# A transformer stack on one core: weight splits moved from the norms' powers into the modulation, one buffer for the normalised activation, five of its blocks made during V

## The chip, the cores and the metric

The kernel runs on one core of a Trainium2 chip. A time is the device time of one launch in microseconds. The kernel before has a median of 1303.39 us over three runs, from 1303.30 to 1306.41 us. The one execution that was profiled took 1308.08 us, and the span of its trace is 1306.3 us. TensorE is called PE, VectorE DVE, ScalarE ACT, GpSimd POOL, and SyncE (which issues the loads here) SP.

## The reference

256 rows of width 1024 pass through two blocks. The first has two layers of three sublayers each, and every sublayer is a norm, a modulation by vectors that come from a conditioning vector, some products, and a gated addition to the residual stream:

```python
def rms_norm(x, g): return x * rsqrt(mean(x * x, -1) + EPS) * g
def modulate(h, shift, scale): return h * (1.0 + scale) + shift
def swiglu(h, w_in, w_out):
    g, u = split(h @ w_in, 2)
    return (silu(g) * u) @ w_out
for layer in range(2):
    mods = split(silu(c) @ ada_w[layer] + ada_b[layer], 9)      # shift, scale, gate of three sublayers
    h = modulate(rms_norm(x, norm_g[layer, 0]), mods[0], mods[1])
    x = x + 0.5 * (1 + mods[2]) * swiglu(h, ffn_w_in[layer, 0], ffn_w_out[layer, 0])
    h = modulate(rms_norm(x, norm_g[layer, 1]), mods[3], mods[4])
    y = pool_mixer(h) if layer == 0 else attention(h, *kv) @ w_o  # windowed means; 8 heads of 128
    x = x + (1 + mods[5]) * y
    h = modulate(rms_norm(x, norm_g[layer, 2]), mods[6], mods[7])
    x = x + 0.5 * (1 + mods[8]) * swiglu(h, ffn_w_in[layer, 1], ffn_w_out[layer, 1])
    if layer == 0:
        k, v = split(modulate(rms_norm(x, kv_norm), *kv_mods) @ w_kv, 2)
        kv = rope(rms_norm(k)), v
```

The second block (one layer) norms and modulates x, multiplies it by a wide w_in, runs a state-space branch and a latent-attention branch, merges them with gates and adds the normed result to x.

## The kernel before, in words

**Tiling.** The residual stream X lies transposed in SBUF as eight blocks of 128 x 256 (width by rows). Every weight is cut into tiles of 128 x 1024 floats (512 KB). SP loads a tile as `wraw` (L215, five buffers); ACT rounds it to `whi` (L229) and DVE subtracts that to get the rest, `wlo` (L220). Activations are split in the same way into the two halves of `hhl`. PE then forms every block product as three: `whi` by high, `wlo` by high, `whi` by low (L355 to L358, L368 to L370). A tile's split is asked for by `Stream.split`, mostly four tiles ahead of its use.

**Modulation vectors.** Each is a product of a 512 KB tile `graw` with the conditioning vector. Most are made on DVE (`junk`, L389), a few on PE while PE would wait in a norm; the table GAPS says which three. Their results come back through three ACT copies (`grow`, L414) and a transposition (L419).

**A norm.** ACT squares the blocks of X, POOL adds them up (L484), PE sums over partitions (L500), DVE adds epsilon (`stm`, L518), POOL takes the power -1/2 (`strs`, L520), and PE spreads the result over the partitions (L526). `st_finish` (L503) does this, and between the power's issue and PE's spreading it calls `more` (L507), which splits one weight tile beyond those already asked for: `whi` on ACT and `wlo` on DVE.

**The modulation** (`modulated`, L541) takes the eight blocks in order. For a block DVE forms `hraw` (L533), ACT adds the shift and rounds (`hhl`, L534), DVE makes the low part (L538), one block behind. At block 2 ACT also makes the three `grow` copies. PE's next products take the blocks in this order.

**The order of the work** is written out by the program: each engine runs its instructions in the order in which the Python calls make them, and waits at the first whose inputs aren't there. A buffer of a pool is given out anew when its last reader is done; `hhl` comes from a pool of one buffer, so a new activation waits for the last product with the old one.

**Places.** The names of norms used below: g00 (after the first FFN, before the pool mixer), gpool (before the second FFN), g01 (before the shared keys and values), g10 (before the attention's queries), g11 (after attention), p2 (before the second block). After the values (V) the first FFN of layer 1 uses the same norm as the keys, kept in `rbs`. The head is the part up to the first FFN's products; there the first tiles and vectors (`hg`) are still being loaded.

Of the kernel before, what the change touches and what calls it, by code (L numbers as in the profile page):

```python
# [8 lines left out]
F32 = mybir.dt.float32  # L9
F32R = mybir.dt.float32r  # L10
# [3 lines left out]
OP = mybir.AluOpType  # L14
# [3 lines left out]
T = 256  # L18
KB = 8
# [46 lines left out]
def _cols(v):  # L66
# [3 lines left out]
NADA = 184  # L70
ADA_PAIR = [m * 8 + k for k in range(8) for m in (0, 1)]
ADA_LAYER = ADA_PAIR + list(range(16, 72))
GAPS = {"g00": (57, 58, 59), "gpool": (64, 65, 66), "g01": (104, 105, 106), "g10": (128, 129, 130),
        "p2": (176, 177, 178), "g11": (152, 153, 154)}
HEAD_PE = {0: (4, 6), 2: (8, 10), 4: (12, 14)}
POOL_PE = (60, 61, 62, 63)
# [174 lines left out]
class Kernel:  # L251
    def __init__(self, nc, tc, h, ctx, dbg=None):
        self.nc, self.tc, self.h, self.ctx = nc, tc, h, ctx
        self.dbg = dbg or {}
        self.bg = deque()
        self.pending = deque()
        self.budget = deque()
        self.small_q, self.small_rate, self.small_credit = deque(), 0.0, 0.0
        self.credit = 0.0
        self.calls = 0  # L260
        self.late = None
        self.lq = []

    def dump(self, name, t):
        if name in self.dbg:
# [237 lines left out]
    def st_finish(self):  # L503
        self.st_reduce()
        if self.gap:
            self.gap[0](2, 5)
            self.more()  # L507
        rb = self.st_spread()
        if self.gap:
            self.gap[0](5, 8)  # L510
        return rb
# [26 lines left out]
        self.nc.vector.scalar_tensor_tensor(a[:, kb, 1], hr, g[:, 1, kb:kb + 1], a[:, kb, 0].bitcast(F32),  # L538
                                            op0=OP.add, op1=OP.subtract)

    def modulated(self, rb, g, a):  # L541
        prev = None
        for kb in range(KB):
            hr = self.mod_a(rb, g, a, kb)
            if kb == 2 and self.gap:
                self.gap[1]()
                self.gap = None
            if prev:
                self.mod_b(*prev)
            prev = (hr, g, a, kb)  # L550
        self.mod_b(*prev)

    def newh(self):
        return self.hpool.tile([128, KB, 2, T], F32R, name="hhl")

    def update(self, kb, ps, g, eng=None, late=None):
        for i in range(0, ps.shape[1], T):
# [208 lines left out]
                                   op0=OP.mult, op1=OP.mult)  # L766
        self.ropeT = {kind: t}

    def kv_project(self, hh):
        nc = self.nc  # L770
        with self.tc.tile_pool(name="kvt", bufs=1) as self.ap:
            self.rope_table(0, "k", 128.0 ** 0.5)
            ssq = self.ap.tile([128, 8, 2], F32, name="kssq")
            pend = []

            def rope(p, nch, th):
                m1 = self.qk_rope(p, nch, th, ssq, "k")
                pend.append(lambda: self.qk_transpose(m1, self.KT, nch, th))

            def evac(nch, pp):  # L780
                while pend:
                    pend.pop(0)()
                if nch < 2:
                    for th in range(2):
                        self.qk_stats(pp[th], nch, th, ssq)
                        self.defer(rope, pp[th], nch, th, lag=1 + th)
                else:
                    for th in range(2):
                        nc.scalar.copy(self.VV[:, th, (nch - 2) * 512:(nch - 1) * 512], pp[th])
            self.proj_b(hh, 4, evac)  # L790

    def attention(self, hh, gate_fn, pre):
        nc, V = self.nc, self.nc.vector
        with self.tc.tile_pool(name="attn", bufs=1) as self.ap:
            self.rope_table(1, "q", 1.0)
            QT = self.ap.tile([128, 8, T], F32, name="QT")
            rq = self.ap.tile([128, 8, 2], F32, name="rq")
            self.shift(self.ap, 192)
            oo = self.ap.tile([128, 8, 2, T], F32R, name="ohl")
            pend = []  # L800

            def evac(nch, pp):
                while pend:
                    pend.pop(0)()
                if nch:
                    last_pp.extend(pp)
                    return
                stats(pp, nch)
                for th in range(2):
                    rope(pp[th], nch, th)  # L810

            def stats(pp, nch):
                for th in range(2):
                    self.qk_stats(pp[th], nch, th, rq)

            def rope(p, nch, th):
                m1 = self.qk_rope(p, nch, th, rq, "q")
                pend.append(lambda: self.qk_transpose(m1, QT, nch, th))
            last_pp = []
            S, P, PT = {}, {}, {}  # L820

            def rest():
                while pend:
                    pend.pop(0)()

            def s1a(h):
                S[h] = self.softmax_a(self.ps("D" if h < 2 else "A"), QT[:, h], self.KT[:, h], 0,
                                      lambda th: rq[:, h, th:th + 1], rq[:, h, :])

            def s1b(h):  # L830
                P[h] = self.softmax_b(*S.pop(h))

            def s2(h):
                PT[h] = self.p_transpose(P.pop(h))

            def s3(h):
                pt = PT.pop(h)
                po = self.ps("D")
                d = slice(h * 128, h * 128 + 128)
                nc.tensor.matmul(po[:, :256], self.VV[:, 0, d], pt[:, :256], start=True, stop=False)  # L840
                nc.tensor.matmul(po[:, 128:256], self.VV[:, 1, d], pt[:, 256:], start=False, stop=True)
                nc.scalar.copy(oo[:, h, 0], po[:, :T])
                V.tensor_sub(oo[:, h, 1], po[:, :T], oo[:, h, 0].bitcast(F32))

            mids = self.gemvs(AT_A, 152)
            first, mids, last = mids[:AT_Q], mids[AT_Q:len(mids) - AT_O], mids[len(mids) - AT_O:]
            self.plan(first, [0] * 3 + [1] * 3)
            self.proj_b(hh, 2, evac, hooks={HQ: rest, (1, 6): lambda: s1a(0)})
            self.drain()
            for it in range(1, 11):  # L850
                if it == 4:
                    rest()
                if it < 8:
                    s1a(it)
                if it - 1 < 8:
                    s1b(it - 1)
                if it == 1:
                    stats(last_pp, 1)
                if 0 <= it - 2 < 8:
                    s2(it - 2)  # L860
                if it < 3:
                    rope(last_pp[it - 1], 1, it - 1)
                if 0 <= it - 3 < 8:
                    s3(it - 3)
                if mids:
                    mids.pop(0)()
            g = gate_fn()
            self.st_begin(KB)

            self.plan(mids + last, [1] * len(mids + last))  # L870
            self.proj_a(oo, lambda n, p: self.update(n, p, g), wide=KB - 1)
            self.drain()
            self.pre = pre()
            self.st_half(D, "g11")
# [38 lines left out]
    def setup(self):  # L913
# [8 lines left out]
        padp = self.pool("pad")  # L922
        self.wraw = self.pool("wraw", bufs=RAWB)
        self.whl = self.pool("whl", bufs=HLB)
        self.last = -1
        self.nraw = GRAW
        self.gend = ADA_POS[179]
# [13 lines left out]
    def phase1(self):  # L941
# [12 lines left out]
        with ExitStack() as p1:  # L954
# [79 lines left out]
            nc.gpsimd.tensor_tensor(warm, warm, self.mhalf[:, 0:2], op=OP.pow)  # L1034
            hgemv(1)
            self.st_reduce()
            hgemv(0)
            self.ws.split(1)
            rb = self.st_spread()
            rbs = self.tmp.tile([128, T], F32, name="rbs", bufs=1)  # L1040
            nc.scalar.copy(rbs, rb)
            hps = self.ps("C")
            g0 = self.small.tile([128, 2, 8], F32, name="gain")
            h0 = self.newh()

            hg = self.small.tile([128, 2, 8], F32, name="gate")
            V.tensor_scalar_add(hg[:, 1], self.adab[:, 1:16:2], 1.0)
            V.tensor_scalar_mul(hg[:, 0], self.cols[:, 0:8], 32.0)
            V.tensor_mul(hg[:, 1], hg[:, 1], hg[:, 0])

            more = [((7, 8, 10), 7), ((9,), 9), ((11, 12, 14), 11), ((13,), 12), ((15,), 14), ((), 16),
                    ((), 18), ((), 19)]
# [2 lines left out]
            def feed(k):  # L1055
                self.ws.ahead = self.ws.depth = 0
                c = slice(k, k + 1)
                los = []
                if k:
                    self.ws.split((14 * k + 21) // 8, los)  # L1060
                if k - 2 in HEAD_PE:
                    V.tensor_add(g0[:, 1, k:k + 2], hps[:, 256:320:32], self.adab[:, 2 * k:2 * k + 3:2])
                    self.done.update(HEAD_PE[k - 2])
                a = slice(2 * k + 1, 2 * k + 2)
                V.scalar_tensor_tensor(g0[:, 0, c], self.modc[:, a], hg[:, 0, c], hg[:, 1, c],
                                       op0=OP.mult, op1=OP.add)
                if k < 2:
                    V.tensor_add(g0[:, 1, c], self.modc[:, 2 * k:2 * k + 1], self.adab[:, 2 * k:2 * k + 1])
                hr = self.mod_a(rbs, g0, h0, k)
                if k:  # L1070
                    los.pop(0)()
                self.mod_b(hr, g0, h0, k)
                if k == 0:
                    self.ws.split(2)
# [32 lines left out]
            for l in range(2):  # L1107
                base = 88 * l
                if l == 0:
                    hh = h0  # L1110
                else:
                    hh = self.newh()
                    g = self.gains(l, 0, 1, 24 * l)
                    self.modulated(rb_next, g, hh)
                if l == 0:
                    self.plan(self.gemvs(16, 64), ffn_plan(2 * LEAD, W_OUT[0]), ssm[0], SLOTS)
                else:
# [22 lines left out]
                if l == 0:  # L1140
# [4 lines left out]
                    hh = self.newh()  # L1145
                    self.modulated(rbs, self.pre, hh)
                    self.plan(self.gemvs(KV_A, 104), KV_W, ssm[2], 16)
                    self.kv_project(hh)
                    self.drain()
                    self.dump("d_KT", self.KT)  # L1150
                    self.dump("d_VV", self.VV)
# [797 lines left out]
```

## Time and profile before

| what | value |
|---|---|
| median of three runs | 1303.39 us (1303.30 to 1306.41) |
| profiled execution, its span | 1308.08 us, 1306.3 us |
| PE busy | 1258.7 us (96% of the span) |
| DVE busy | 1015.6 us (78%) |
| ACT busy | 669.4 us (51%) |
| POOL busy | 165.3 us (13%) |
| mean granted clock of PE | 0.987 |
| moved by DMA | 331.14 MB, mean 253 GB/s |

PE is the engine with the least idle time; its stretches without work are short and stand at few places. The granted clock says which share of 2.4 GHz PE was given. Idle time of the other engines matters only where PE waits for them.

### The profile page before, as it was taken

The page shows a single profiled execution, that of the slowest core. Times are in us where ns is not written, and L with a number is a line of the kernel's source. Part 1 is how long each engine was busy: PE and PEld are TensorE (multiplying, and loading weights), DVE is VectorE, ACT ScalarE, POOL GpSimd, SP SyncE. Part 2 cuts the span into 40 slices and gives each one's busy share as a digit, 9 for nine tenths or more (in the row PEclk, how much of TensorE's full clock was granted, in tenths as well). Part 3 has the DMA queues.
Part 4 walks back from the last instruction along what each step waited for, and adds up shares of the span by engine and source line. Part 5 has one row for each costly group of instructions (what it writes and reads, how often), then busy time and mean ns, then how long its engine had stood idle before and what let it go on. Part 6 is the DMA issues. An engine that isn't in the chain of part 4 may idle for free.

```text
span 1306.3 us, 25415 instructions
## 1 busy us (share of the span) xinstructions
PE 1258.7 (96%) x9870; PEld 1167.4 (89%) x9870; DVE 1015.6 (78%) x1768; ACT 669.4 (51%) x1170; POOL 165.3 (13%) x285
## 2 busy tenths in 40 slices
PE   7999999999999999999998999999999899989998
PEld 5999988899988779999886899998888888989997
DVE  6789896789999789999977777878853576537774
ACT  4455444555444665544447555444465855437443
POOL 1000011100002000121111201000210791100000
PEclk9999999899999999999999999999998999989999
DMA  9899996788899568998974478778655544764852
GB/s 365 297 344 386 335 369 237 251 310 259 274 326 332 203 256 299 312 324 301 360 279 145 129 237 268 265 258 282 223 195 172 156 130 124 226 202 143 292 191 81
DMA packets 119850, 331.14 MB, mean 253 GB/s; under 512 B 28273, under 2 KB 39409, under 8 KB 119666
## 3 DMA queue, kind: packets, MB, share of 16 engines
q1 hardware_dynamic: 119730, 329.52, 73.4%
q8 instruction: 77, 1.26, 0.4%
q14 instruction: 43, 0.35, 0.1%
HBM read 317.94 MB, written 10.49 MB: 251 GB/s over the span
## 4 chain that ended last, share of the span: by engine, by line
PE 71%; DVE 4%; ACT 4%; issue 2%; DMA 2%; POOL 1%; SPq 0%; DVEq 0%; ACTq 0%; POOLq 0%
PE psD L356 13%; PE psB L356 12%; PE psA L356 11%; PE psC L356 7%; PE psA L363 5%; PE psB L363 4%; PE psA L364 3%; PE psB L364 2%; DVE wlo L220 1%; PE psA L368 1%; PE psA L369 1%; PE psA L370 1%; PE psB L368 1%; PE psB L370 1%; PE psB L369 1%
## 5 line engine op out<-in xcount | busy, mean ns | idle before, releaser
L220 DVE TENSOR_TENSOR wlo<-wraw,whi 128x1024 fp32r<-128x1024 f32 x391 | 481.3, 1236 | 44.6 <-ACT whi L229 43.4
L229 ACT CAST whi<-wraw 128x1024 fp32r<-128x1024 f32 x391 | 403.1, 1049 | 94.5 <-ACT whi L229 32.7
L356 PE MATMUL psA<-hhl,whi 128*128 128x256 f32 x960 | 247.4, 283 | 4.7 <-ACT hhl L534 4.6
L356 PE MATMUL psB<-hhl,whi 128*128 128x256 f32 x976 | 248.4, 281 | 0.0
L356 PE MATMUL psD<-hhl,whi 128*128 128x256 f32 x1120 | 213.7, 283 | 0.4 <-ACT hhl L534 0.4
L356 PEld LDWEIGHTS psA<-hhl,whi 128*128 128x128 f32 x960 | 180.2, 189 | 7.9 <-ACT hhl L534 6.2
L356 PEld LDWEIGHTS psB<-hhl,whi 128*128 128x128 f32 x976 | 183.8, 190 | 0.0
L389 DVE SCALAR_TENSOR_TENSOR junk<-graw,cb 128x1024 bf16<-128x1024 f32 x146 | 179.3, 1228 | 5.5 <-DMA cb<-in_c 5.5
L356 PEld LDWEIGHTS psD<-hhl,whi 128*128 128x128 f32 x1120 | 178.6, 190 | 2.7 <-issue 1.8
L356 PE MATMUL psD<-hhl,wlo 128*128 128x256 f32 x560 | 157.2, 281 | 0.0
L356 PE MATMUL psB<-hhl,wlo 128*128 128x256 f32 x488 | 136.9, 281 | 0.0
L356 PE MATMUL psA<-hhl,wlo 128*128 128x256 f32 x480 | 134.9, 281 | 1.3 <-DVE wlo L220 1.3
L363 PE MATMUL psA<-shl,whi 128*128 128x512 f32 x352 | 123.8, 392 | 0.0
L356 PEld LDWEIGHTS psD<-hhl,wlo 128*128 128x128 f32 x560 | 106.3, 190 | 0.0
L364 PE MATMUL psA<-shl,wlo 128*128 128x256 f32 x352 | 99.2, 282 | 0.0
L356 PE MATMUL psC<-hhl,whi 128*128 128x256 f32 x480 | 93.4, 286 | 0.4 <-DVE hhl L1456 0.4
L356 PEld LDWEIGHTS psA<-hhl,wlo 128*128 128x128 f32 x480 | 91.2, 190 | 1.7 <-DVE wlo L220 1.7
L356 PEld LDWEIGHTS psB<-hhl,wlo 128*128 128x128 f32 x488 | 92.4, 189 | 0.0
L363 PE MATMUL psB<-shl,whi 128*128 128x512 f32 x264 | 92.2, 390 | 0.0
L484 POOL TENSOR_TENSOR stacc<-stacc,stsq 128x256 f32<-128x256 f32 x33 | 35.1, 1063 | 381.9 <-ACT stsq L479 340.4
L356 PEld LDWEIGHTS psC<-hhl,whi 128*128 128x128 f32 x480 | 77.0, 191 | 3.2 <-issue 2.2
L363 PEld LDWEIGHTS psA<-shl,whi 128*128 128x128 f32 x352 | 66.1, 188 | 14.3 <-issue 0.8
(453 smaller groups left out, 2362.1 us busy)
## 6 DMA issues: line engine op xcount, KB each, us to landing
wraw<-in_win SPq DMA_DIRECT2D x176, 512.0 KB
graw<-in_ada SPq DMA_DIRECT2D x173, 512.0 KB
wraw<-in_w SPq DMA_DIRECT2D x93, 512.0 KB
wraw<-in_wout SPq DMA_DIRECT2D x88, 512.0 KB
wraw<-in_wkv SPq DMA_DIRECT2D x16, 512.0 KB
hg<-in_ada SPq DMA_DIRECT2D x11, 512.0 KB
Hd<-ct SPq DMA_DIRECT2D x64, 64.0 KB
Gd<-gsb SPq DMA_DIRECT2D x16, 256.0 KB
```

What stands on the lines that cost most here:

```text
L220: self.nc.vector.tensor_sub(lo, raw, hi.bitcast(F32))
L229: self.nc.scalar.copy(hi, raw)
L356: self.nc.tensor.matmul(*a, skip_group_check=shared, **kw)
L363: mm(out, hi[:, b], a.rearrange("p x t -> p (x t)"), start=first, stop=False)
L364: mm(out[:, :T], lo[:, b], a[:, 0], start=False, stop=last)
L368: mm(out, ah, whi, start=first, stop=False)
L369: mm(out, ah, wlo, start=False, stop=False)
L370: mm(out, al, whi, start=False, stop=last)
L389: self.nc.vector.scalar_tensor_tensor(junk, self.gemv_tile(j), 1.0, self.cb, op0=OP.mult, op1=OP.mult, accum_out=self.modc[:, j:j + 1])
L484: (eng or nc.gpsimd).tensor_add(acc, acc, sq)
```

## The change

Six edits. The three vectors that PE makes at g01 are others (101 to 103 in place of 104 to 106), so that DVE makes three fewer during the keys and values and three more in the next FFN. `more` is no longer called in `st_finish`; a flag is set there, and `modulated` calls it after the low part of block 1. `hhl` is one tile for the whole program. During the last quarter of V five blocks of the next FFN's activation are made, the other three after V. In attention's output the square of block 6 is added by DVE and not by POOL. In the head some small operations and the copy of the norm go ahead of a vector product and of the second weight tile's split, and a weight tile is loaded later.

```diff
-        "g01": (104, 105, 106), "g10": (128, 129, 130),
+        "g01": (101, 102, 103), "g10": (128, 129, 130),
...
         if self.gap:
             self.gap[0](2, 5)
-            self.more()
+            self.owed = True
         rb = self.st_spread()
...
-    def modulated(self, rb, g, a):
+    def modulated(self, rb, g, a, kbs=range(KB)):
         prev = None
-        for kb in range(KB):
+        for kb in kbs:
             hr = self.mod_a(rb, g, a, kb)
             if kb == 2 and self.gap:
                 self.gap[1]()
                 self.gap = None
             if prev:
                 self.mod_b(*prev)
+            if kb == 2 and self.owed:
+                self.more()
+                self.owed = False
             prev = (hr, g, a, kb)
         self.mod_b(*prev)

     def newh(self):
-        return self.hpool.tile([128, KB, 2, T], F32R, name="hhl")
+        if self.H is None:
+            self.H = self.hpool.tile([128, KB, 2, T], F32R, name="hhl")
+        return self.H
...
-    def kv_project(self, hh):
+    def kv_project(self, hh, then):
...
-            self.proj_b(hh, 4, evac)
+            self.proj_b(hh, 4, evac, hooks={(3, 6): then})
...
-            self.proj_a(oo, lambda n, p: self.update(n, p, g), wide=KB - 1)
+            self.proj_a(oo, lambda n, p: self.update(n, p, g, nc.vector if n == 6 else None), wide=KB - 1)
...
-            hgemv(0)
-            self.ws.split(1)
-            rb = self.st_spread()
-            rbs = self.tmp.tile([128, T], F32, name="rbs", bufs=1)
-            nc.scalar.copy(rbs, rb)
             hps = self.ps("C")
...
+            scale0(0)
+            hgemv(0)
+            rb = self.st_spread()
+            rbs = self.tmp.tile([128, T], F32, name="rbs", bufs=1)
+            nc.scalar.copy(rbs, rb)
+            lo0 = []
+            self.ws.split(1, lo0)
...
-                los = []
+                los = [] if k else lo0
...
-                if k:
-                    los.pop(0)()
+                los.pop(0)()
                 self.mod_b(hr, g0, h0, k)
...
-                    g = self.gains(l, 0, 1, 24 * l)
-                    self.modulated(rb_next, g, hh)
+                    self.modulated(rb_next, nxt[0], hh, range(5, KB))
...
-                    self.kv_project(hh)
+                    nxt = []
+
+                    def first_half():
+                        nxt.append(self.gains(1, 0, 1, 24))
+                        self.modulated(rbs, nxt[0], hh, range(5))
+                    self.kv_project(hh, first_half)
```

On DVE at the norm after the first FFN, g00, the order before was this (`stm` is the sum with epsilon, `wlo` a weight tile's rest):

```order
215 L518 TENSOR_SCALAR stm<-psC 128x2
216 L220 TENSOR_TENSOR wlo<-wraw,whi 128x1024
217 L533 SCALAR_TENSOR_TENSOR hraw<-X,gain,psC 128x256 x2
218 L538 SCALAR_TENSOR_TENSOR hhl<-hraw,gain,hhl 128x256
219 L533 SCALAR_TENSOR_TENSOR hraw<-X,gain,psC 128x256
220 L538 SCALAR_TENSOR_TENSOR hhl<-hraw,gain,hhl 128x256
221 L533 SCALAR_TENSOR_TENSOR hraw<-X,gain,psC 128x256
```

And now, on DVE at the same place:

```order
215 L519 TENSOR_SCALAR stm<-psC 128x2
216 L534 SCALAR_TENSOR_TENSOR hraw<-X,gain,psC 128x256 x2
217 L539 SCALAR_TENSOR_TENSOR hhl<-hraw,gain,hhl 128x256
218 L534 SCALAR_TENSOR_TENSOR hraw<-X,gain,psC 128x256
219 L539 SCALAR_TENSOR_TENSOR hhl<-hraw,gain,hhl 128x256
220 L220 TENSOR_TENSOR wlo<-wraw,whi 128x1024
221 L534 SCALAR_TENSOR_TENSOR hraw<-X,gain,psC 128x256
```

The subtraction stood ahead of all blocks and now stands between the low part of block 1 and the `hraw` of block 3. The other five norms read alike.

On ACT at the same norm, before (`stlast` is the last square, `grow` the copies of PE's vectors):

```order
103 L471 ACTIVATE stlast<-X 128x256
104 L229 CAST whi<-wraw 128x1024
105 L534 ACTIVATE hhl<-hraw,gain 128x256 x3
106 L414 COPY grow<-psC 1x128 x3
107 L534 ACTIVATE hhl<-hraw,gain 128x256 x5
```

And now on ACT:

```order
103 L472 ACTIVATE stlast<-X 128x256
104 L535 ACTIVATE hhl<-hraw,gain 128x256 x3
105 L415 COPY grow<-psC 1x128 x3
106 L229 CAST whi<-wraw 128x1024
107 L535 ACTIVATE hhl<-hraw,gain 128x256 x5
```

The rounding of the weight tile went from ahead of the first block to behind the three copies, after block 2.

On ACT at the end of V, before (`VV` is the copy of a finished piece of V):

```order
236 L789 COPY VV<-psB 128x512
237 L229 CAST whi<-wraw 128x1024 x4
238 L789 COPY VV<-psA 128x512
239 L789 COPY VV<-psB 128x512
240 L534 ACTIVATE hhl<-hraw,gain 128x256 x8
```

And now on ACT at the end of V:

```order
236 L795 COPY VV<-psB 128x512
237 L229 CAST whi<-wraw 128x1024 x3
238 L535 ACTIVATE hhl<-hraw,gain 128x256 x5
239 L229 CAST whi<-wraw 128x1024
240 L795 COPY VV<-psA 128x512
241 L795 COPY VV<-psB 128x512
242 L535 ACTIVATE hhl<-hraw,gain 128x256 x3
```

Five of the eight blocks are now rounded ahead of the last two copies of V, with one weight tile behind them.

On SP in the head, before (`hg` is a vector's tile):

```order
14 L992 DMA hg_167<-in_ada 128x1024
15 L215 DMA wraw<-in_win 128x1024 x2
16 L992 DMA hg_244<-in_ada 128x1024
17 L992 DMA hg_246<-in_ada 128x1024
18 L992 DMA hg_248<-in_ada 128x1024
19 L215 DMA wraw<-in_win 128x1024
```

And now on SP in the head:

```order
14 L999 DMA hg_167<-in_ada 128x1024
15 L215 DMA wraw<-in_win 128x1024
16 L999 DMA hg_242<-in_ada 128x1024
17 L999 DMA hg_244<-in_ada 128x1024
18 L999 DMA hg_246<-in_ada 128x1024
19 L215 DMA wraw<-in_win 128x1024 x2
```

One weight tile went from ahead of three vectors' tiles to behind them.

## Rows read from the trace of the kernel before

**Rows 1.** The chain that ended last, shares of the span by engine (profile page).

```profile
PE 71%; DVE 4%; ACT 4%; issue 2%; DMA 2%; POOL 1%; SPq 0%; DVEq 0%; ACTq 0%; POOLq 0%
```

**Rows 2.** Timeline of POOL, powers of norms: start, us, instruction, count, idle before it, releaser.

```profile
10.63 1.66 POOL L520 TENSOR_TENSOR strs<-stm,mhalf 128x2 f32<-128x2 f32 x1 [1.23 <-DVE stm L518]
...
212.88 0.70 POOL L520 TENSOR_TENSOR strs<-stm,mhalf 128x2 f32<-128x2 f32 x1 [6.18 <-ACT whi L229]
...
235.10 1.62 POOL L520 TENSOR_TENSOR strs<-stm,mhalf 128x2 f32<-128x2 f32 x1 [1.17 <-DVE stm L518]
...
751.00 1.61 POOL L520 TENSOR_TENSOR strs<-stm,mhalf 128x2 f32<-128x2 f32 x1 [1.53 <-DVE stm L518]
```

**Rows 3.** Timeline of DVE at the norm after the first FFN.

```profile
212.91 1.24 DVE L220 TENSOR_TENSOR wlo<-wraw,whi 128x1024 fp32r<-128x1024 f32 x1
214.10 0.87 DVE L533 SCALAR_TENSOR_TENSOR hraw<-X,gain,psC 128x256 f32<-128x256 f32 x2
...
216.59 0.48 DVE L533 SCALAR_TENSOR_TENSOR hraw<-X,gain,psC 128x256 f32<-128x256 f32 x1
...
221.38 0.48 DVE L538 SCALAR_TENSOR_TENSOR hhl<-hraw,gain,hhl 128x256 fp32r<-128x256 f32 x1 [0.18 <-ACT hhl L534]
```

**Rows 4.** Timeline of ACT at the same norm.

```profile
211.85 1.03 ACT L229 CAST whi<-wraw 128x1024 fp32r<-128x1024 f32 x1
...
216.61 0.80 ACT L414 COPY grow<-psC 1x128 f32<-1x128 f32 x3
...
223.05 0.58 ACT L678 COPY pz<-psB 128x512 f32<-128x512 f32 x1
```

**Rows 5.** Timeline of PE at the same norm, first product of the pool mixer.

```profile
224.46 0.67 PE L694 MATMUL psA<-pm,pz 128*128 128x256 f32 x2 [1.44 <-DMA pm<-in_k_pool]
```

**Rows 6.** Timeline of SP's issues at the same norm.

```profile
216.17 0.42 SPq L664 DMA_DIRECT2D pm<-in_k_pool  x1
```

**Rows 7.** Timeline of DVE, low part of block 2 at three later norms.

```profile
240.39 0.48 DVE L538 SCALAR_TENSOR_TENSOR hhl<-hraw,gain,hhl 128x256 fp32r<-128x256 f32 x1
...
434.12 0.48 DVE L538 SCALAR_TENSOR_TENSOR hhl<-hraw,gain,hhl 128x256 fp32r<-128x256 f32 x1
...
680.55 0.48 DVE L538 SCALAR_TENSOR_TENSOR hhl<-hraw,gain,hhl 128x256 fp32r<-128x256 f32 x1
```

**Rows 8.** Timeline of PE, first product with block 2's low part at these norms.

```profile
243.86 0.28 PE L356 MATMUL psA<-hhl,whi 128*128 128x256 f32 x1
...
435.82 0.40 PE L370 MATMUL psA<-whi,hhl 128*128 128x512 f32 x1
436.06 0.40 PE L368 MATMUL psB<-whi,hhl 128*128 128x512 f32 x1
...
682.26 0.40 PE L370 MATMUL psA<-whi,hhl 128*128 128x512 f32 x1
```

**Rows 9.** Timeline of DVE in the shared keys, a modulation product.

```profile
464.03 1.22 DVE L389 SCALAR_TENSOR_TENSOR junk<-graw,cb 128x1024 bf16<-128x1024 f32 x1
```

**Rows 10.** Timeline of PE, waits in the keys and after the values.

```profile
466.45 0.50 PE L369 MATMUL psA<-wlo,hhl 128*128 128x512 f32 x1 [1.40 <-DVE wlo L220]
...
482.44 0.39 PE L356 MATMUL psA<-hhl,whi 128*128 128x256 f32 x1 [1.08 <-ACT hhl L534]
```

**Rows 11.** Timeline of PE, a wait near the start of the second block.

```profile
976.74 1.01 PE L500 MATMUL psC<-ones,stacc 128*128 128x1 f32 x4 [2.09 <-ACT stacc L473]
```

**Rows 12.** Windows: stretch, length, busy PE PEld DVE ACT POOL, granted clock, DMA share, GB/s.

```profile
233.00:243.50 10.50, 8.98 (x74) 7.57 (x75) 7.38 (x18) 4.82 (x12) 2.56 (x3) 0.67 0.53 201
...
961.00:977.00 16.00, 13.67 (x112) 13.07 (x110) 7.96 (x11) 15.81 (x22) 0.00 (x0) 0.99 0.66 230
977.00:987.00 10.00, 10.00 (x42) 8.92 (x43) 3.79 (x6) 3.49 (x6) 2.29 (x2) 0.50 0.35 105
```

**Rows 13.** Timeline of ACT in the head.

```profile
24.98 1.05 ACT L229 CAST whi<-wraw 128x1024 fp32r<-128x1024 f32 x1 [0.29 <-DMA wraw<-in_win]
...
29.05 0.51 ACT L534 ACTIVATE hhl<-hraw,gain 128x256 fp32r<-128x256 f32 x1 [3.03 <-DVE hraw L533]
```

More of the change, by code (lines that the diff above doesn't have):

```diff
@@ L72 @@
 ADA_LAYER = ADA_PAIR + list(range(16, 72))
-GAPS = {"g00": (57, 58, 59), "gpool": (64, 65, 66), "g01": (104, 105, 106), "g10": (128, 129, 130),
+GAPS = {"g00": (57, 58, 59), "gpool": (64, 65, 66), "g01": (101, 102, 103), "g10": (128, 129, 130),
         "p2": (176, 177, 178), "g11": (152, 153, 154)}
@@ L549, in modulated @@
                 self.mod_b(*prev)
+            if kb == 2 and self.owed:
+                self.more()
+                self.owed = False
             prev = (hr, g, a, kb)
@@ L924, in setup @@
         self.whl = self.pool("whl", bufs=HLB)
+        self.H = None
         self.last = -1
@@ L1049, in phase1, with scale0 @@
             V.tensor_mul(hg[:, 1], hg[:, 1], hg[:, 0])
+            def scale0(k):
+                V.scalar_tensor_tensor(g0[:, 0, k:k + 1], self.modc[:, 2 * k + 1:2 * k + 2], hg[:, 0, k:k + 1],
+                                       hg[:, 1, k:k + 1], op0=OP.mult, op1=OP.add)
+            scale0(0)
[5 more added lines that the diff above has]
+            self.ws.split(1, lo0)
             more = [((7, 8, 10), 7), ((9,), 9), ((11, 12, 14), 11), ((13,), 12), ((15,), 14), ((), 16),
@@ L1063, in feed @@
                     self.done.update(HEAD_PE[k - 2])
-                a = slice(2 * k + 1, 2 * k + 2)
-                V.scalar_tensor_tensor(g0[:, 0, c], self.modc[:, a], hg[:, 0, c], hg[:, 1, c],
-                                       op0=OP.mult, op1=OP.add)
+                if k:
+                    scale0(k)
                 if k < 2:
```

## The prediction

> **What bounds the kernel now.** I read the chain that ended last first: PE holds 71% of it, DVE and ACT 4% each, POOL 1% [rows 1]. So only work that PE waits for counts. Then I looked for PE's idle stretches in its timeline, and for what the other engines did around each norm. A norm is the place where PE has little of its own to do. The reader is to see three things. First, the power on POOL takes 0.70 us where it begins ahead of the weight tile's subtraction on DVE (212.88 against 212.91) and 1.61 to 1.66 us at three other places, where a DVE instruction had begun [rows 2, 3]. Second, between the power and the first block DVE and ACT have a hole, and the extra weight split lies in it: at g00 `whi` begins at 211.85, `wlo` ends at 214.15, and the first `hraw` begins at 214.10, as soon as the norm is spread [rows 3, 4]. Third, from then on DVE is the slow member: eight blocks from 214.10 to the last low part at 221.38, 0.91 us a block [rows 3], and PE's first products wait for them.
>
> **The split in the modulation.** This is the main term. It occurs six times. At g00 the three `grow` copies on ACT begin at 216.61 and last 0.80, so they end at 217.41. `whi` now stands behind them and takes 1.03: 218.44. `wlo` then takes 1.24, and the next instruction on DVE may start some 0.04 before that ends: about 219.65 [rows 3, 4]. That next one is the `hraw` of block 3, which before began at 216.59. So **every DVE instruction from block 3 on, and the low part of block 2 behind it, comes 3.06 us later**. What is taken out ahead gains nothing at g00: `hraw` already began when the norm was there. Queued behind the waiting `wlo` on DVE are five blocks; behind `whi` on ACT are five roundings that wait for DVE in any case. Who waits for the blocks differs from place to place.
>
> *g00.* The pool mixer needs all eight blocks, the last low part was at 221.38, the last copy `pz` began at 223.05 and lasted 0.58 (end 223.63) [rows 3, 4]. PE's next product began at 224.46, but that waited for the load of `pm` [rows 5], issued by SP at 216.17 [rows 6], 8.3 us earlier. The copy now ends at about 223.63 + 2.98 = 226.61 (DVE's last block makes up 0.08 on its wait for ACT): **+2.15**. SP issues a weight tile's load ahead of `pm`, and that load needs the buffer that the moved `wlo` frees at 219.65; `pm` then leaves some 4 us later, and with the same 8.3 us its product begins at 228.5. Bounds: 0, if the eighth block hides the delay, and +4.0; I take 2.15, by the rows of ACT, since fewer loads are in flight there then.
>
> *gpool.* The power begins at 235.10 and takes 1.62; without a `wlo` beside it 0.70, so everything begins 0.92 earlier [rows 2]. Then the low part of block 2, which began at 240.39, comes at 240.39 - 0.92 + 3.06 = 242.53, and ends at 243.01. PE's first product with it was at 243.86 [rows 7, 8], and PE is at half clock for most of that stretch (granted 0.67 from 233 to 243.5) [rows 12]. So about 0.75 of the 0.92 stays, a little less for the handover: **-0.6**. Bounds -1.7 (all of it, and the half clock ends earlier) and +0.3.
>
> *g01 and g10.* The low part of block 2 began at 434.12 and 680.55. It would end at 434.12 + 3.06 + 0.48 = 437.66 and at 684.09. PE's first product with it was at 435.82 and at 682.26 [rows 7, 8], and PE has nothing else queued that is ready. **+1.83 and +1.83** (I write 1.9 for the second, whose transposition stands closer). After that PE spends six products of 0.24 us (435.82 to 436.06) on a block, 1.4 us, and DVE 0.91, so no further wait arises. Bounds: 0 and 3.06 each.
>
> *g11.* Again the power was long, 1.61 [rows 2]. The addition of block 6's square moves from POOL to DVE and puts `stm` some 0.4 us later. 0.92 - 0.4, less a little that block 2 takes back: **-0.3**, bounds -0.9 and +1.
>
> *p2.* Here ACT is the slow member: from 961 to 977 it is busy 15.81 of 16.00 us [rows 12], and PE's wait of 2.09 us that ends at 976.74 is for ACT's `stacc` at the end of that chain [rows 11]. The chain starts when the last block is rounded, so all 3.06 go through: **+3.0**. The stretch behind it runs at half clock already [rows 12]; a longer wait may move its end by 1.5 either way.
>
> **Keys, values and the FFN behind them.** DVE's product at 464.03 (1.22 us) stands ahead of the `wlo` for which PE waits 1.40 us until 466.45 [rows 9, 10]. It is one of the three that leave the keys and values: **-1.25**, bounds 0 and -1.57 (with its handover). They come back in the FFN of layer 1, between the splits on DVE, which is idle 22% of the span; nothing is charged, and without that cover it would be 3 x 1.22 = 3.7 us. At the end of V PE waits 1.08 us for the first rounded block, until 482.44 [rows 10]; this block is now made during V, and with the handover **-1.25** goes, bounds 0 and -1.5. What is late next there are blocks 5 to 7, which PE reaches only after five blocks' products of 1.4 us or more. The one tile for `hhl` makes this possible and costs nothing else: its parts are written after the products that read them.
>
> **Head.** The power took 1.66 us, since a vector product ran beside it [rows 2]; about 0.9 us of that goes. But here loads set the pace: ACT, which needs 1.05 us for a weight tile, waits another 0.29 for one at 24.98, so tiles come 1.34 us apart, and DVE's `hraw` of block 2 keeps ACT waiting until 29.05 [rows 13]. The tile that now lies behind three vectors' loads comes about 3 x 1.34 = 4.0 us later, at 29.0; its rounding stands on ACT ahead of block 2's, which then begins at 30.05 and not at 29.05. The vectors come earlier in return, and `hraw` with them. I take **0**: bounds -1.5 (the power's gain is carried on, and the vectors' too) and +1.0 (block 2 late by what the row says).
>
> **The sum.** 2.15 - 0.6 + 1.83 - 1.25 - 1.25 + 1.9 - 0.3 + 3.0 + 0 = **+5.5 us**. The profiled execution took 1308.08, so it would be 1313.6 in such a one; the median of the runs is 1303.39, 4.7 below the profiled one, and the shift put on that gives **1308.9**.
>
> **A rule weighed.** The Trainium skill, "SBUF — State Buffer" (the part on reading the port diagram), says that DVE and POOL share one pair of ports as an exclusive lock: who starts first holds it for the whole instruction. The first rows agree in one direction (1.61 to 1.66 against 0.70), and not in the other: the `wlo` that began 0.03 us after the power took 1.24 us, no longer than others. By the rule in both directions `wlo` beside the power would have cost DVE 0.7 us at g00, and taking it away would be worth up to that much there; by the row it is worth nothing.
>
> **The rivals.** A measurement of this kernel tells a difference of about 0.3%, 3.9 us, from none: below 1299.5 is faster, above 1307.3 slower.
>
> *Same mechanism, smaller.* The waits at block 2 are partly covered, because SP's loads or PE's vector products run into them, and the head carries its 1.5 through: 5.5 - 1.5 - 1.9 = +2.1, or **1305.5**. For it: gaps on PE at norms hold spare products. Against it: at g01 and g10 these stand ahead of the blocks.
>
> *The other side: the cover holds.* The low part of block 2 is not what PE waits for, since PE's 1.4 us of products per block against DVE's 0.91 leaves a store of work when `wlo` comes. It is decided at one point, whether that low part is there before PE's third product of block 2. If it is, only the gains stay: -0.6 - 0.3 - 1.25 - 1.25 = -3.4, and with the head's -1.5, -4.9: **1298.5 to 1300**. For it: gpool, where half clock gives such a store. Against it: at g01 and g10 the store is 435.82 - 434.60, 1.2 us, and 3.06 are wanted.
>
> *The clock falls.* The new waits at g01 and g10 come on top of those the norm has already, and if a stretch there went down to 1.2 GHz, as from 977 to 987 (granted 0.50) [rows 12], each 3.4 us of it would cost 1.7. Two such stretches: 5.5 + 3.4 = +8.9, **1312.3**. For it: gpool and p2 show such stretches. Against it: g01 and g10 show none now. The Trainium skill, "TensorE: Matmul & The Clock Gate" (part 1), says that an idle array falls back to the lower clock, which speaks for this rival; no run here shows it at these two places.
>
> *The powers stay long.* If DVE's small operations hold POOL as `wlo` did, the 0.92 at gpool and half of that at g11 stay: +0.9 to the sum, **1309.8**.
>
> **How the numbers follow.** Forecast 0.48 (its own range 1306.5 to 1311.5; 0.08 of the 0.48 lie within 0.3%); smaller 0.18 (no change); the other side 0.20 (0.15 faster, 0.05 no change); the clock 0.09 and the powers 0.05, both slower. Faster 0.15; no change 0.08 + 0.18 + 0.05 = 0.31; slower 0.40 + 0.09 + 0.05 = 0.54. The range runs from 1300.5, which leaves out the better half of the other side, to 1312, which leaves out part of the clock's.
>
> **What would show it.** In the profile after: at every norm a hole of about 2 us on DVE between the low part of block 1 and `wlo`, ended by `whi`; PE idle 1.8 us within the first three blocks at g01 and g10; PE's wait near 976.74 at 5 us in place of 2.09; powers of 0.7 us at gpool and g11; no wait at the start of layer 1's first FFN, nor for the `wlo` in the keys. The forecast is wrong if the hole on DVE is there and PE has no wait behind it, or if PE's total idle time falls.

## The result, and the profile after

The changed kernel takes 1315.53 us (median of four runs, 1314.61 to 1318.96) against 1303.35 us for the kernel before (1301.05 to 1306.41): a ratio of 1.0099, 95% interval 1.0077 to 1.0122. It is slower by 12.2 us, where 5.5 were forecast and 1312 was the end of the range. Direction and main mechanism held; the size did not. The granted clock does not make the difference: at 0.989 three runs of the changed kernel (a0 below) took 1314.32 to 1315.93 us, and four of the kernel before on the same chip 1302.39 to 1305.92.

The main mechanism is written in one line of the costliest groups on the profile pages (busy and mean ns of one, then idle time of DVE just before, and what ended it). First the second profile of before, then after:

```profile
L220 DVE TENSOR_TENSOR wlo<-wraw,whi 128x1024 fp32r<-128x1024 f32 x391 | 480.3, 1234 | 43.6 <-ACT whi L229 42.9
```

```profile
L220 DVE TENSOR_TENSOR wlo<-wraw,whi 128x1024 fp32r<-128x1024 f32 x391 | 481.0, 1235 | 56.5 <-ACT whi L229 56.2
```

The same 391 subtractions at the same length, but DVE waits 13 us longer ahead of them, for `whi`: six times 2 us (1.93 to 2.05 in the timeline). The timeline of DVE at g00 after shows one of the six, where [rows 3] showed none:

```profile
214.62 0.87 DVE L534 SCALAR_TENSOR_TENSOR hraw<-X,gain,psC 128x256 f32<-128x256 f32 x2 [1.30 <-PE psC L527]
...
219.03 1.23 DVE L220 TENSOR_TENSOR wlo<-wraw,whi 128x1024 fp32r<-128x1024 f32 x1 [1.96 <-ACT whi L229]
220.17 0.47 DVE L534 SCALAR_TENSOR_TENSOR hraw<-X,gain,psC 128x256 f32<-128x256 f32 x1
...
224.88 0.48 DVE L539 SCALAR_TENSOR_TENSOR hhl<-hraw,gain,hhl 128x256 fp32r<-128x256 f32 x1 [0.18 <-ACT hhl L535]
```

From the first `hraw` to that of block 3 it is 5.55 us, against 216.59 - 214.10 = 2.49 in [rows 3]: 3.06 more, as worked out. Who pays is seen in the timeline of PE after, at g00, gpool, g01, g10, g11 and p2 in turn (idle before, and releaser, in brackets):

```profile
221.10 0.39 PE L371 MATMUL psB<-whi,hhl 128*128 128x256 f32 x1 [2.64 <-DVE hhl L539]
...
246.13 0.39 PE L357 MATMUL psA<-hhl,whi 128*128 128x256 f32 x1 [1.30 <-DVE hhl L539]
...
440.59 0.50 PE L371 MATMUL psA<-whi,hhl 128*128 128x512 f32 x1 [1.70 <-DVE hhl L539]
...
446.73 0.50 PE L370 MATMUL psA<-wlo,hhl 128*128 128x512 f32 x1 [0.52 <-DVE wlo L220]
...
686.57 0.50 PE L371 MATMUL psA<-whi,hhl 128*128 128x512 f32 x1 [1.68 <-DVE hhl L539]
...
692.69 0.50 PE L370 MATMUL psA<-wlo,hhl 128*128 128x512 f32 x1 [0.50 <-DVE wlo L220]
...
764.60 0.38 PE L357 MATMUL psA<-hhl,whi 128*128 128x256 f32 x1 [1.08 <-DVE hhl L539]
...
966.25 0.50 PE L357 MATMUL psD<-hhl,whi 128*128 128x256 f32 x2 [0.95 <-DVE hhl L539]
...
972.25 0.38 PE L357 MATMUL psB<-hhl,wlo 128*128 128x256 f32 x1 [0.87 <-DVE wlo L220]
```

At all six norms PE now waits for block 2's low part, from 0.95 to 2.64 us; the products of [rows 8] at g01 and g10 wait 1.7 us. Six microseconds later PE waits once more, for the `wlo` of the next tile: 0.5 us at g01 and g10, 0.87 at p2. That second wait was not in the forecast.

The gains came too. The powers of [rows 2] are short on POOL:

```profile
10.54 0.71 POOL L521 TENSOR_TENSOR strs<-stm,mhalf 128x2 f32<-128x2 f32 x1 [1.23 <-DVE stm L519]
...
238.07 0.70 POOL L521 TENSOR_TENSOR strs<-stm,mhalf 128x2 f32<-128x2 f32 x1 [1.17 <-DVE stm L519]
...
756.71 0.70 POOL L521 TENSOR_TENSOR strs<-stm,mhalf 128x2 f32<-128x2 f32 x1 [4.59 <-DVE stm L519]
```

Of the two waits of [rows 10], the one after V is gone, and the one in the keys is a rest of 0.25:

```profile
470.52 0.50 PE L370 MATMUL psA<-wlo,hhl 128*128 128x512 f32 x1 [0.25 <-DVE wlo L220]
```

### The profile page after: what moved, and what is told of

It reads as the page before. It is cut to its first block, busy times and chain, and to the rows that moved or that the text cites. A ratio compares the mean times of both kernels' runs of the same rounds, so it can differ in the third digit from the quotient of the medians.

```text
span 1313.1 us, 25416 instructions
## 1 busy us (share of the span) xinstructions
PE 1261.0 (96%) x9870; PEld 1166.8 (89%) x9870; DVE 1013.7 (77%) x1769; ACT 668.6 (51%) x1170; POOL 153.0 (12%) x284
## 4 chain that ended last, share of the span: by engine, by line
PE 68%; DVE 6%; ACT 4%; issue 3%; DMA 1%; POOL 1%; SPq 0%; DVEq 0%; ACTq 0%; POOLq 0%
PE psD L357 12%; PE psB L357 12%; PE psA L357 11%; PE psC L357 7%; PE psA L364 5%; PE psB L364 4%; PE psA L365 3%; DVE wlo L220 2%; PE psB L365 2%; PE psA L369 1%; PE psA L370 1%; PE psA L371 1%; PE psB L371 1%; PE psB L370 1%; PE psB L369 1%
## 5 line engine op out<-in xcount | busy, mean ns | idle before, releaser
L601 ACT CAST shl<-sf 128x256 fp32r<-128x256 f32 x88 | 35.8, 407 | 88.6 <-DVE sf L599 88.6
```

What stands on the lines that cost most here:

```text
L601: nc.scalar.copy(ss[:, i, 0], s)
```

## The experiments

Ratios are to the kernel before on the same chip, with 95% intervals. The experiments ran on three chips, on which the median of before was 1303.79 to 1304.59 us. To see where the microseconds lie, I also took for each trace the start of the same PE instruction at some marks. The table gives its lateness in us against the second profile of before (span 1301.8); the first column is the first profile of before (span 1306.3). The runs are named as at the experiments below.

| mark, us in the first trace of before | before, first | after | e2 move only | e1 split back | c2 |
|---|---|---|---|---|---|
| 40, head done | +1.0 | +1.5 | +0.1 | +2.6 | -0.3 |
| 214, before g00 | +1.1 | +1.6 | -0.4 | +2.1 | +0.3 |
| 224.4, pool mixer | +1.1 | +3.9 | +2.0 | +0.6 | -1.0 |
| 260, behind gpool | +1.2 | +4.1 | +1.9 | -0.5 | -3.4 |
| 425, before g01 | +0.2 | +3.1 | +1.0 | -1.5 | -4.4 |
| 442, behind g01 | +0.2 | +5.8 | +3.7 | -1.5 | -4.1 |
| 490, behind V | +0.2 | +2.6 | +3.8 | -4.7 | -7.3 |
| 690, behind g10 | +0.2 | +5.3 | +6.5 | -4.7 | -7.3 |
| 740, before g11's norm | +0.8 | +6.2 | +6.6 | -3.6 | -5.6 |
| 752.6, behind g11's power | +0.8 | +5.6 | +5.6 | -3.3 | -6.2 |
| 760, behind g11 | +2.4 | +7.8 | +7.6 | -2.7 | -6.2 |
| 950, before p2 | +2.5 | +7.9 | +7.8 | -2.7 | -6.8 |
| 977.4, behind p2 | +2.9 | +10.9 | +11.0 | -2.7 | -6.8 |
| 1299, end | +4.5 | +11.3 | +10.2 | -4.3 | -6.5 |

**Before, once more (e0).** No edit.

> The kernel before, unchanged, run and profiled once more. The two profiled executions differ by 6.8 us in span, the medians by 12.2. Theory 1 (the profiled execution of before was a slow one of its kind): span now 1299 to 1302, and the half-clock stretches are other or fewer than in the first profile. Rival (an execution with a profile is always longer than the others for this kernel): span again near 1306. Time 1303 in either case.

1303.88 us, 1.0005 (0.9988 to 1.0021). The second profile has a span of 1301.8, 4.5 less than the first, so theory 1 holds: the profiled execution on which the forecast's sum stood was a long one of its kind. Windows of the first profile, around g11 and p2 (stretch, length, busy PE, PEld, DVE, ACT, POOL, granted clock, DMA share, GB/s):

```profile
749.00:764.00 15.00, 13.19 (x125) 11.86 (x117) 12.92 (x27) 8.82 (x16) 2.08 (x2) 0.89 0.62 214
960.00:1000.00 40.00, 37.67 (x304) 34.07 (x302) 18.10 (x27) 26.79 (x41) 2.98 (x3) 0.87 0.53 179
```

And of the second:

```profile
749.00:764.00 15.00, 13.19 (x131) 12.09 (x132) 12.92 (x27) 9.81 (x17) 1.61 (x1) 1.00 0.67 222
960.00:1000.00 40.00, 36.13 (x304) 32.45 (x302) 18.35 (x25) 27.81 (x43) 2.98 (x3) 0.91 0.51 170
```

The same kernel ran g11 with a stretch at 1.2 GHz once and wholly at 2.4 GHz the other time, and stayed at 1.2 GHz for less of the stretch behind p2. By the table that is 1.6 us at g11 (from 740 to 760), and 1.5 from 950 to 990 us, where the first is 4.0 behind. Another 0.6 lies between g10 and g11; the 1.0 of the head is down to 0.2 by g01. The stretch at g11 matters for the split too. Block 2's low part on DVE and PE's first product with it, at g11, in the first profile:

```profile
756.02 0.48 DVE L538 SCALAR_TENSOR_TENSOR hhl<-hraw,gain,hhl 128x256 fp32r<-128x256 f32 x1
...
759.31 0.28 PE L356 MATMUL psA<-hhl,whi 128*128 128x256 f32 x1
```

And in the second:

```profile
755.19 0.48 DVE L538 SCALAR_TENSOR_TENSOR hhl<-hraw,gain,hhl 128x256 fp32r<-128x256 f32 x1
...
756.95 0.28 PE L356 MATMUL psA<-hhl,whi 128*128 128x256 f32 x1
```

The low part was there 2.8 us ahead of PE in the one and 1.3 in the other.

**The split back (e1).** After, with one line changed:

```diff
-            self.owed = True
+            self.more()
```

> After, but the weight split stands beside the power again, as before; all other edits stay. Theory 1 (the moved split costs all of it): the gain at keys, values and the next FFN stays, so 1303.4 - 2.5 = 1301, with no hole on DVE before wlo. Rival (other edits, the head or the reused tile, carry about 5 of the 12.2 us): 1305 to 1308.

1300.99 us, 0.9975 (0.9962 to 0.9988). Theory 1. That its figure is met to the microsecond is luck: before took 1304.59 on this chip, so by the ratio the gain is 3.3 us and not 2.5. All other edits together are a small gain.

**The move alone (e2).** Before, with the split moved as in the change (flag in the norm, call behind the low part of block 1) and nothing else.

```diff
...
-            self.more()
+            self.owed = True
...
+            if kb == 2 and self.owed:
+                self.more()
+                self.owed = False
```

> Before, with the move of the split alone. The six norms shift by +2.0, +0.7, +2.7, +2.5, +0.2 and +1.4 us in the trace of after against before, in sum 9.5. Theory 1 (the moved split costs more than the net, 12.2 + 2.5): 1316 to 1318. Rival (it costs what the two traces show, the rest lies in other edits): 1312 to 1313.

1316.10 us, 1.0085 (1.0068 to 1.0103). The time is theory 1's, the difference is not: by the ratio the move costs 11.1 us (8.9 to 13.4), nearer to the rival's 9.5 than to the 14.7 of theory 1, which lies outside the interval. The move alone makes the kernel about as slow as the whole change does. By the table it costs 2.4 at g00, 0 at gpool (the short power pays for the blocks), 2.7 at g01, 2.7 at g10, 1.0 at g11 (the blocks cost 2.0, the short power gives 0.9) and 3.2 at p2, in sum 12; 1.7 of it comes back between gpool and g01 and behind p2. PE at g11 in this trace:

```profile
764.40 0.38 PE L357 MATMUL psA<-hhl,whi 128*128 128x256 f32 x1 [1.67 <-DVE hhl L539]
```

**Keys and values alone (e3).** Before, with the vectors at g01, the one tile, and five blocks made during V (as in the change's diff).

```diff
+            self.proj_b(hh, 4, evac, hooks={(3, 6): then})
...
+                    self.modulated(rb_next, nxt[0], hh, range(5, KB))
```

> Before, with three edits alone: the vectors at g01, one tile for the activation, five blocks made during V. Theory 1: the two waits of 1.40 and 1.08 us are gone, 1303.4 - 2.5 = 1300.9. Rival (the five blocks and DVE's three products cost as much elsewhere): 1303 to 1306.

1300.76 us, 0.9967 (0.9954 to 0.9980). Theory 1's time; 3.8 us below the median of before on this chip, where it expected 2.5. The traces of after, e1 and this kernel all show 3.2 us between the marks 442 and 490, a little over the 2.5 of the forecast.

**After, once more (a0).** No edit.

> After, unchanged, measured beside the others. Theory 1 (the edits add up: the move +11.5 us as measured alone, the keys and values -3.8, head and the rest about 0): 1304 + 8 = 1312. Rival (head, block 6's square and the rest cost 4 us where the split is moved, or the two interact): 1315 to 1317.

1315.47 us, 1.0084 (1.0067 to 1.0100). The rival's figure. Moved split and keys alone make +11.1 and -4.3 us by their ratios, the head +1.6 (below), in sum 8.4; after is +11.0 here and +12.9 in the first measurement. Within the changed kernel the move makes 14.2 (this ratio less that of e1). The intervals are each 1.7 to 2.9 us to either side, so an interaction is not shown, and none is excluded. The square of block 6 was not tried alone.

**The split behind the eighth block (e4).**

```diff
-            if kb == 2 and self.owed:
-                self.more()
-                self.owed = False
             prev = (hr, g, a, kb)
         self.mod_b(*prev)
+        if self.owed:
+            self.more()
+            self.owed = False
```

> After, with the extra split behind the eighth block and not inside the modulation. Theory 1 (the blocks' delay of 3.06 us is what costs, and a second wait of 0.5 to 0.8 us for the next tile's wlo): no hole between blocks; the next wlo comes about 1.2 us later than in the split-back kernel, some 0.8 us at four norms, powers short, 1301 + 3 - 1.8 = 1302 to 1304. Rival (what costs is that the split left the hole beside the power, wherever it goes): 1312 or more.

1324.43 us, 1.0155 (1.0138 to 1.0172). My theory missed by 20 us, and the rival is nearer. PE in this kernel, at g00 and at g01:

```profile
229.71 1.19 PE L700 MATMUL psA<-pm,pz 128*128 128x256 f32 x2 [6.02 <-DMA pm<-in_k_pool]
...
446.84 0.50 PE L369 MATMUL psA<-whi,hhl 128*128 128x512 f32 x1 [1.13 <-ACT whi L229]
448.10 0.50 PE L370 MATMUL psA<-wlo,hhl 128*128 128x512 f32 x1 [0.76 <-DVE wlo L220]
...
454.42 0.79 PE L370 MATMUL psA<-wlo,hhl 128*128 128x512 f32 x1 [3.26 <-DVE wlo L220]
```

SP's issues there:

```profile
224.24 0.33 SPq L215 DMA_DIRECT2D wraw<-in_win  x1
224.62 0.43 SPq L670 DMA_DIRECT2D pm<-in_k_pool  x1
...
448.07 0.33 SPq L215 DMA_DIRECT2D wraw<-in_wkv  x1
...
448.93 0.42 SPq L769 DMA_DIRECT2D kqg<-in_kqg  x1
```

And DVE at g01:

```profile
452.47 0.76 DVE L771 SCALAR_TENSOR_TENSOR ropec<-ropec,kqg 128x256 f32<-128x256 f32 x2 [4.43 <-DMA kqg<-in_kqg]
```

Two things stand behind the split. The tile that is split there is the very next that PE wants after the one it holds. And SP issues a new weight tile's load right behind it, which waits for the buffer that this `wlo` frees; the small loads `pm` and `kqg` are queued behind that load, `kqg` holds DVE, and three tiles' `wlo` stand behind it. At g00 `pm` leaves SP at 224.62, 8.4 us later than in [rows 6], and PE waits 6.02 for it. No run issues the small loads ahead of the weight tile, so how much of the 20 us is SP's queue is not shown.

**whi beside the power, wlo inside the modulation (f2).**

```diff
...
-            self.owed = True
+            if self.ws.ns < self.ws.nh + HLB - 1:
+                self.ws.split(self.ws.ns + 1, self.owed)
...
-            if kb == 2 and self.owed:
-                self.more()
-                self.owed = False
+            while kb == 2 and self.owed:
+                self.owed.pop(0)()
```

> After, with the tile's rounding (whi) on ACT beside the power as before and only wlo inside the modulation. Theory 1: the hole of 1.96 us on DVE is gone, the blocks come 1.15 us late in place of 3.06; at g01 and g10 the low part of block 2 is then just in time (435.75 against 435.82), 0.3 at g00, 1.2 at p2, the second wait stays at about 0.8 twice: 1303 to 1304. Rival (a wlo inside the modulation costs what it does by its place, not by its wait for whi): 1309 or more.

1303.13 us, 0.9993 (0.9983 to 1.0002). Theory 1. DVE at g00:

```profile
216.83 0.48 DVE L540 SCALAR_TENSOR_TENSOR hhl<-hraw,gain,hhl 128x256 fp32r<-128x256 f32 x1
217.22 1.22 DVE L220 TENSOR_TENSOR wlo<-wraw,whi 128x1024 fp32r<-128x1024 f32 x1
218.36 0.47 DVE L535 SCALAR_TENSOR_TENSOR hraw<-X,gain,psC 128x256 f32<-128x256 f32 x1
```

No hole; `wlo` starts as the low part ends. Of the 3.06 us 1.9 are the wait for `whi`, which ACT rounds 5 us earlier here (at 212.60, and at 217.96 after); taking that wait away takes away 12 us. PE's only wait behind g01 is 0.44 for the next `wlo`.

**whi beside the power, wlo behind the eighth block (f9).** As the one before, with the `while` loop behind the last block's low part.

> After, with whi beside the power and wlo behind the eighth block: no block is late, no power is long, and only the next tile's wlo is 1.2 us later. Theory 1: 1301 - 1.8 + 2 to 3 = 1301 to 1302, the same as with the split back beside the power. Rival: 1305 or more, if the second wait grows to 1.2 us or more at each norm.

1323.42 us, 1.0146 (1.0129 to 1.0164). Missed as e4 was, and by the trace for the same cause: it is not the rounding but the late `wlo`, with SP's queue behind it. `pm` leaves SP at 224.74 and PE waits 5.64 us for it; DVE waits 4.47 for `kqg`.

**The head alone (e5).** Before, with the head's edit only.

> Before, with the head's edit alone. Theory 1 (the later weight tile makes block 2 about 1 us late and more behind it, taken back at g00 where PE waited 1.4 us for the load of pm): PE 1.5 to 2.5 us later than before at 40 us, the wait at the pool mixer's first product gone, time 1304 to 1305. Rival (the head's delay stays to the end): 1306. Rival (no cost at all): at 40 us as before, 1303.5.

1306.53 us, 1.0012 (0.9999 to 1.0025): no difference clear of noise, 1.6 us at the middle; the first rival's 1306 is nearest. At the 40 us mark PE is 1.5 later than in the second trace of before, but the wait for `pm` is still there (1.53), so the part of theory 1 on where it is taken back is wrong. ACT in this kernel's head:

```profile
29.10 1.05 ACT L229 CAST whi<-wraw 128x1024 fp32r<-128x1024 f32 x1 [4.74 <-DMA wraw<-in_win]
30.05 0.50 ACT L534 ACTIVATE hhl<-hraw,gain 128x256 fp32r<-128x256 f32 x1
```

**The head with the load in its old place (h1).**

```diff
                 los.pop(0)()
+                if k == 0:
+                    self.ws.dma(6)
                 self.mod_b(hr, g0, h0, k)
```

> The head's edit alone, but the sixth weight tile's load back ahead of the three vectors' loads. Theory 1 (the load's place is what makes the head late): PE at 40 us no later than before, perhaps 0.9 earlier by the short power; time 1302.5 to 1303.5. Rival (the order on ACT and DVE, rounding behind the norm's copy, makes it late): PE at 40 us again 1.5 to 2.5 later.

1301.90 us, 0.9978 (0.9965 to 0.9992), PE 1.0 earlier than the second trace of before at 40 us. Theory 1, and 0.6 us below its range. ACT in this head:

```profile
24.72 1.05 ACT L229 CAST whi<-wraw 128x1024 fp32r<-128x1024 f32 x1 [0.31 <-DMA wraw<-in_win]
27.07 0.51 ACT L534 ACTIVATE hhl<-hraw,gain 128x256 fp32r<-128x256 f32 x1 [1.30 <-DVE hraw L533]
```

The sixth tile is rounded 4.4 us earlier than with the load moved, and block 2 at 27.07 in place of 30.05, 2 us ahead even of [rows 13]. So at this mark the rest of the head's edit is worth 1 us, and the load's place costs 2.5.

**Split back and load back (c1).** After, with the edits of e1 and h1.

> After with the split back beside the power and the sixth tile's load back in its place. Theory 1: 1301.0 less what the load cost, 1300 to 1300.5, if PE's wait for pm at g00 does not take the place of the head's delay; with it 1301. Rival: 1303 or more.

1301.47 us, 0.9976 (0.9959 to 0.9992). The rival's 1303 lies at the upper edge of the interval. The gain of 2.5 in the head is not seen in the time: against e1 no difference. 1.5 of it goes as the expectation allowed: PE waits 1.46 us for `pm` at g00 in this trace, and not at all in that of e1. Its profiled execution (span 1304.7) had more at 1.2 GHz than others, mean clock 0.985.

**wlo late at two norms (c2).** As c1, but at gpool and g11 `wlo` goes inside the modulation, with `whi` beside the power (one line of the edit):

```diff
+                self.ws.split(self.ws.ns + 1, self.owed if self.key in ("gpool", "g11") else None)
```

> As the one before, but at the two norms with a long power, gpool and g11, whi alone stands beside the power and wlo comes after block 1. Theory 1: the power is 0.7 there, the blocks from 3 on 1.15 - 0.92 = 0.2 late and hidden, so 0.7 gained at each against the one before: about 1.4 less. Rival (the next tile's wlo is waited for, 0.5 at each, and PE's clock decides): no difference, 1300 to 1301.

1297.01 us, 0.9935 (0.9918 to 0.9952): 0.65% faster than before, some 1.5% faster than after by the two ratios, the fastest of all. It gained 4.5 on c1 where I expected 1.4. The powers take 0.70, and in the profiled execution no stretch at 1.2 GHz stands at gpool or g11. Windows around both:

```profile
222.00:242.00 20.00, 18.54 (x215) 16.02 (x215) 13.94 (x32) 11.11 (x27) 3.54 (x5) 1.00 0.63 237
738.00:758.00 20.00, 18.87 (x182) 17.16 (x181) 16.44 (x32) 12.42 (x21) 2.44 (x3) 1.00 0.59 210
```

Granted 1.00 in both, where before had 0.67 in the shorter stretch of [rows 12]. The clock of every run is on record, and half or more of the 4.5 goes with it: all six runs of c2 were granted 0.991, the twelve of c1 0.985 to 0.992, on average 0.988. The two runs of c1 that were granted 0.991 and 0.992 took 1298.88 and 1297.32 us, against a mean of 1296.7 for c2; at a like clock the gain is some 0.6 to 2.2 by these two, around the 1.4 expected. That the short powers bring the higher clock is not shown: f2 has them too, and a stretch at half clock at gpool.

## Why the forecast was wrong, point by point

The mechanism was right, and sizes failed, of two kinds. The base was one long execution, and the shift worked out on it was put on the median; this is most of the 6.7 us that are missing, and the term at g11 is part of it. And "no further wait arises" at g01 and g10: each measures 2.7, 0.8 to 0.9 more than forecast.

- *The split in the modulation: every block from 3 on 3.06 us later.* Right; measured 3.06 at g00, with the hole of 1.96 ended by `whi`. e1 and e2 show that the move carries the whole loss, f2 that most of it goes with the wait for `whi`.
- *g00, +2.15.* Right in size (between the marks 214 and 224.4 after loses 2.3, e2 2.4), wrong in place, so luck in part. The forecast went by the last copy `pz`; PE waits 2.64 at block 2's low part, and but for 0.27 its products keep it busy from then on. `pm` left SP at 220.66 and was not late: PE had no wait there, and the 1.44 of [rows 5] was saved.
- *p2, +3.0.* Right in size (3.0 after, 3.2 in e2), wrong in place: the wait at 976.74 stayed at 2.09 us; the time went in waits of 0.95 and 0.87 us and smaller ones ahead of it. That the sizes agree is luck.
- *g01 and g10, +1.83 and +1.9.* Mis-sized: 2.7 each. The failed step is "no further wait arises". The first wait is 1.7 us, as worked out. But DVE, 3 us late with the blocks, was late with the next tile's `wlo` as well, and PE waited 0.5 six microseconds on; the other 0.5 of the 2.7 stands at no wait that the profile names. The blocks' consumer had slack; the next instruction behind the blocks on DVE had none.
- *gpool, -0.6.* Measured about 0.1. PE's first product with block 2's low part came 0.5 earlier against before, near the forecast, and followed that part by 0.06. But it was PE that waited, 1.30 us: it had been at 1.2 GHz for less of the stretch (granted 0.84 from 235.8 to 246.3, where [rows 12] have 0.67). The rest is the same second wait, 0.5 later in all.
- *g11, -0.3.* From the mark 740 to 760 it is +1.6 against the second trace of before, which had no half-clock stretch there, and 0.0 against the first, which had. The power gave its 0.9. The mis-sized term is "a little that block 2 takes back": PE waits 1.08 for block 2's low part after, and 1.67 in e2, wholly at 2.4 GHz. The part was 2.8 us ahead of PE in the first trace of before, where PE was at half clock, which nearly covers the 3.06 that the move adds; in the second it was 1.3 ahead. I took what one profiled execution had for what the kernel has.
- *Keys, values, next FFN, -2.5.* Measured -3.2 in three traces, and 3.8 us between the medians of e3 and before.
- *Head, 0.* Measured +1.5 at 40 us in after and in e5, up to 2.6 in e1 (the unchanged head gave 0.0 to 1.0). The weight tile landed at 29.04, as worked out (29.0), and block 2 was rounded at 29.99 (30.05 worked out): the upper bound was the right row, and I set a gain against it that the same load kept from coming.
- *The sum and its base.* The step that failed most: "4.7 below the profiled one, and the shift put on that". The two profiled spans differ by 6.8 us, close to the 5.5. But the profiled execution of before lay 4.7 us above its median and that of after (1315.25) on its own, so the same shift counted from the median is 12. The mean granted clock was 0.987 in that execution of before, 0.990 in the second and 0.989 after; 0.003 of the span is 3.9 us. Part of what before spent at 1.2 GHz in that one execution stood in my base as if the change kept it.
- *The rivals.* The cover did not hold. The clock rival named g01 and g10; the new stretch at half clock came at g00 (granted 0.89 from 213 to 229) instead. The powers are short, so the change does what it says.

The six norms' terms make 8.0 us; the marks of e2 make 12, and its time 11.1 (interval 8.9 to 13.4). What the marks have over the terms is g01 and g10 (1.7), g11 (1.3), gpool (0.5) and 0.4 at g00 and p2.

## What to carry to other kernels

When work is moved into a chain, follow the delay past the first consumer: also the next instruction in line on each late engine, and each load queued on SP behind one that waits for a buffer, can be late. Split a moved step into its halves; here the half on ACT had a free place ahead, and leaving it there made the move cost 2 us (0.9993 of before against 0.9975) and not 14 (1.0084). And a sum made on one profiled execution needs a second one of the same kernel, before its distance to the median is carried over.

## What the runs showed that was not expected

- The same program had its half-clock stretches at different norms from one execution to the next: at g11 granted 0.89 or 1.00 for the same instructions, 1.6 us apart. The changed kernel did the same: from 25 to 45 us, in the head, and from 749 to 769, at g11, it was granted 1.00 and 0.91 in the one profile (after), 0.91 and 1.00 in the other (a0).
- A `wlo` that is later by less than one modulation (from behind block 1 to behind block 8, with `whi` early) turned 1303.13 into 1323.42 us.
